# A hybrid block on one core: weights and small parameters laid out by the host, one piece per partition and transfer

## The chip, the core and the metric

The kernel runs on one core of a Trainium2 chip. The core has TensorE (PE in the profile), VectorE (DVE), ScalarE (ACT), GpSimd (POOL) and SyncE (SP), an on-chip memory of 128 partitions, an accumulation memory that PE writes, and 16 DMA engines that serve the transfers issued from the queues of SP, ACT and POOL. The metric is the device time of one execution in microseconds (us), the median over runs.

## The reference

A block of a diffusion transformer on 1024 latent tokens and 256 context tokens of width 1024, in float32. Cut to what matters:

```python
mod = silu(c) @ w_ada + b_ada                     # six rows of 1024: shift, scale, gate, twice
h = layer_norm(x) * (1 + sc1) + sh1               # the same for the context rows
proj = concat(h_ctx, h_x) @ w_in                  # 1024 x 3088: q, k, v, z, beta, decay, rx, ry
q, k, v = silu(conv4(q, k, v))                    # depthwise convolution over 4 tokens
o = gated_delta_rule(q, k, v, beta, decay)        # 4 heads, both directions, chunks of 64 tokens
hr = rg_lru(conv4(rx), wa, ba, wi, bi, lam)       # linear recurrence, both directions
u = concat(rmsnorm(o) * silu(z), hr * gelu(ry)) @ w_out
x = layer_norm(2**0.25 * x + gt1 * u) * g0 + b0
hm = layer_norm(x) * (1 + sc2) + sh2
y = sum over the two chosen experts e of 32:      # one group of four, then the top two in it
        weight[e] * (silu(hm @ gate[e]) * (hm @ up[e])) @ down[e]
out = layer_norm(2**0.25 * x + gt2 * y) * g1 + b1
```

The experts' weights are the bulk of what is read: 32 x (1024 x 256 gate, 1024 x 256 up, 256 x 1024 down), 96 MB.

## The kernel before, in words

One function, `hybrid_block`, builds the whole program. The order of the instructions on each engine is planned when the program is built, from a simulated timeline, and kept at run time.

**Head (0 to 85 us).** `c` and `c_ctx` are loaded as rows (L178, L179), passed through Silu, transposed by PE and copied to `cT`. `ada_rows` (L198) loads the first 2048 columns of `w_ada` in four transfers of 2 MB (tile `wada`, two buffers) and multiplies. The bias `b_ada` is loaded as rows `br` and transposed too (L213 to L217). The rows of x come on ACT's queue behind the third and fourth of these transfers. `wbd` (L239 to L241) holds 16 columns of `w_in` in 64-byte rows. Then come the layer norm, transposes and the split of h into a high and a low part (`hhi`, `hlo`). `stg` (L293 to L303) gathers 92 rows of small parameters in six transfers and transposes them into `par`; `dtb` (L305 to L307) takes two broadcasts.

**Projections, delta rule and recurrence (85 to 575 us).** `proj_cm` (L407) loads 128 columns of `w_in` (24 times 512 KB, in rows of 512 bytes), splits them and multiplies. `ada_late` loads the rest of `w_ada` in 32 transfers of 512 KB. `rg_gates` (L740) sets `wg` to zero on POOL and fills its diagonal blocks with four transfers, four times.

**Scan and output (575 to 853 us).** `prepare` (L925) loads `w_out` in eight transfers on SP's queue and after them the router's weights in two (L941, L942), the first with 16-byte rows, the second with 128-byte rows. `scan_step`, `rest` and `finish` run the delta rule over chunks, the output projection, the norms and the router's logits.

**Experts (853 to 1240 us).** Token and expert pairs are packed into 24 blocks of 128 places, of which some hold parts of two or four experts. For each block POOL gathers rows of `h2d` (L1449), PE transposes them, `up` (L1471) multiplies with gate and up side by side (`w`, 8 values of k, 512 columns), `down` (L1492) with the down weights (`d`), DVE scales the result into `y` (three buffers), and POOL adds it row by row into `acc` in DRAM (L1496): one scatter for each expert part of the block, 39 in all. Each of these scatters waits until the one before has landed, since they add into the same tensor. `load_w` (L1373) and `load_d` (L1380) bring the weights on SP's queue into six buffers for `w` and five for `d`; `behind` lets each load start only when the one two places before it has landed.

**End (1240 to 1279 us).** `acc` is read back, normalised and written out.

Of the kernel before, what the change touches and what calls it, by code (L numbers as in the profile page):

```python
# [9 lines left out]
F32 = mybir.dt.float32  # L10
# [8 lines left out]
P = 128  # L19
D = 1024  # L20
# [67 lines left out]
def hybrid_block(ctx, tc, x, c, ctx_in, c_ctx, w_ada, b_ada, w_in, conv_qkv_w, dn_a_log, dn_dt_bias, dn_onorm_w,  # L88
         rg_conv_w, rg_conv_b, rg_wa, rg_ba, rg_wi, rg_bi, rg_lambda, w_out, ln_g, ln_b,
         router_wg, router_bg, router_we, router_be, w_e_gate, w_e_up, w_e_down, ranks, only, out):  # L90
# [86 lines left out]
    cc = sb.tile([16, P], F32, name="cc", tag="cc")  # L177
    nc.sync.dma_start(cc[0:8, :], c[0].rearrange("(k p) -> k p", p=P))  # L178
    nc.sync.dma_start(cc[8:16, :], c_ctx.rearrange("(k p) -> k p", p=P))  # L179
# [14 lines left out]
    w_ada_v = w_ada[0].rearrange("(k p) n -> p k n", p=P)  # L194
# [45 lines left out]
    nc.vector.memset(wbd, 0.0)  # L240
    nc.scalar.dma_start(wbd[:, :, 0:16], w_in[0].rearrange("(k p) n -> p k n", p=P)[:, :, 2048:2064])  # L241
# [53 lines left out]
    nc.scalar.dma_start(stg[48:64, :], rg_conv_w[0].rearrange("j (t p) -> (j t) p", p=P))  # L295
    nc.scalar.dma_start(stg[64:68, :], rg_conv_b[0].rearrange("(t p) -> t p", p=P))
    nc.scalar.dma_start(stg[68:76, :], rg_ba[0].rearrange("d (t p) -> (d t) p", p=P))
    nc.scalar.dma_start(stg[76:84, :], rg_bi[0].rearrange("d (t p) -> (d t) p", p=P))
    nc.scalar.dma_start(stg[84:92, :], rg_lambda[0].rearrange("d (t p) -> (d t) p", p=P))
    pp = pm()  # L300
# [83 lines left out]
    w_in_v = w_in[0].rearrange("(k p) n -> p k n", p=P)  # L384

# [21 lines left out]
    def proj_cm(col, ctx_too):  # L407

        hi, lo = split_w(w_in_v[:, :, col:col + P], KT, P)
# [513 lines left out]
    w = {}  # L923
# [730 lines left out]
```

## Time and profile before

| | us |
|---|---|
| median of 3 runs | 1289.57 |
| lowest and highest of them | 1284.93, 1298.79 |
| the profiled execution | 1280.62 |
| its span, first to last instruction | 1278.9 |
| PE busy in it | 1112.5 (87%) |
| DVE busy | 682.3 (53%) |
| ACT busy | 422.4 (33%) |
| POOL busy | 424.9 (33%) |

The profile is one execution. A line of the timeline gives the start, the duration, engine, line of the program, operation, output and inputs, and in brackets how long the engine was idle before and what ended that. The chain of waits is followed back from the last instruction, at each step to what released it; "SPq" is a DMA issue on SP's queue, "issue" is time in which nothing that the profile shows was waited for. The share of the DMA engines is the sum of the packets' durations over 16 engines; it can come out a little above 1. q1 is SP's queue, q10 ACT's, q0 POOL's.

### The profile page before, as it was taken

What the parts mean: (1) busy time and instruction counts of PE and PEld (TensorE: products, weight loads), DVE (VectorE), ACT (ScalarE), POOL (GpSimd) and SP (SyncE); (2) the same over time, 40 slices, a digit from 0 to 9 for tenths busy, and PEclk for the clock granted to TensorE, in tenths of its full rate; (3) what the DMA queues carried; (4) which work ended last, traced back from release to release, by engine and by line L of the source; (5) the groups of instructions that cost most, each with busy time, mean ns of one, the idle gap of its engine ahead of it and who ended that gap; (6) DMA issues with size and microseconds to landing.
All of it is one profiled execution on the core that took longest, in us unless ns stands there. A gap on an engine that the chain in (4) does not pass through costs nothing.

```text
span 1278.9 us, 18429 instructions
## 1 busy us (share of the span) xinstructions
PE 1112.5 (87%) x6810; PEld 701.4 (55%) x6810; DVE 682.3 (53%) x1570; ACT 422.4 (33%) x755; POOL 424.9 (33%) x492
## 2 busy tenths in 40 slices
PE   4799998998999989987999999984898999999720
PEld 1357775776767677665667777772323433443210
DVE  3737479487684975875446766654211322222227
ACT  0535324233321727971222446540211212112003
POOL 1511414232242223353640176841211322222225
PEclk8799999999897999996999999975999999999975
DMA  9413453645536231009886255349999999999955
GB/s 335 163 49 93 140 149 94 189 139 140 141 111 160 69 104 37 17 19 306 266 256 214 93 188 185 114 186 332 336 332 355 342 309 307 308 311 315 314 178 169
DMA packets 208883, 251.43 MB, mean 197 GB/s; under 512 B 37276, under 2 KB 164440, under 8 KB 208792
## 3 DMA queue, kind: packets, MB, share of 16 engines
q1 hardware_dynamic: 194128, 215.94, 53.0%
q0 software_dynamic: 7888, 16.80, 5.7%
q10 hardware_dynamic: 6776, 17.50, 3.5%
q8 instruction: 54, 0.88, 0.3%
q14 instruction: 37, 0.30, 0.1%
HBM read 206.39 MB, written 55.20 MB: 205 GB/s over the span
## 4 chain that ended last, share of the span: by engine, by line
PE 39%; DMA 29%; DVE 17%; issue 6%; POOL 3%; SPq 3%; ACT 3%; DVEq 0%; POOLq 0%; ACTq 0%
DMA w<-in_w_e_up_dram 8%; DMA acc<-y,tbri 5%; PE pj L403 4%; PE pj L405 4%; PE pj L404 4%; DMA acc<-y,rows_to 4%; DMA d<-in_w_e_down_dram 4%; DVE s L621 4%; DVE s L619 4%; DMA wada<-in_w_ada_dram 2%; PE pu L1471 2%; PE p L1148 2%; PE pf L403 2%; PE pf L405 2%; PE pf L404 2%
## 5 line engine op out<-in xcount | busy, mean ns | idle before, releaser
L1471 PE MATMUL pu<-w,xT 128*32 128x512 f32 (+2 forms) x848 | 189.1, 614 | 19.0 <-DMA w<-in_w_e_up_dram 17.0
L403 PE MATMUL pj<-hhi,whi 128*128 128x512 f32 (+1 forms) x480 | 188.6, 393 | 4.5 <-ACT s L439 2.8
L404 PE MATMUL pj<-hlo,whi 128*128 128x512 f32 (+1 forms) x480 | 185.9, 387 | 0.0
L405 PE MATMUL pj<-hhi,wlo 128*128 128x512 f32 (+1 forms) x480 | 184.3, 385 | 0.0
L1471 PEld LDWEIGHTS pu<-w,xT 128*32 128x32 f32 (+2 forms) x848 | 61.8, 135 | 116.9 <-issue 104.0
L403 PEld LDWEIGHTS pj<-hhi,whi 128*128 128x128 f32 x480 | 92.5, 193 | 49.6 <-issue 18.6
L399 POOL TENSOR_TENSOR wlo<-wraw,whi 128x1024 fp32r<-128x1024 f32 x21 | 52.8, 2513 | 155.2 <-ACT whi L398 87.3
L405 PEld LDWEIGHTS pj<-hhi,wlo 128*128 128x128 f32 x480 | 92.7, 193 | 20.8 <-issue 5.7
L1492 PE MATMUL py<-d,hT 128*32 128x512 f32 (+2 forms) x424 | 101.0, 598 | 3.1 <-DMA d<-in_w_e_down_dram 2.1
L404 PEld LDWEIGHTS pj<-hlo,whi 128*128 128x128 f32 x480 | 92.8, 193 | 19.3 <-issue 5.3
L1474 DVE TENSOR_TENSOR hid<-hid,pu 128x256 f32<-128x256 f32 x24 | 10.0, 421 | 138.0 <-ACT hid L1473 138.0
L1496 POOL DMA_INDIRECT acc<-y,rows_to x28 | 41.3, 1476 | 116.4 <-DMA acc<-y,rows_to 51.0
L619 DVE TENSOR_TENSOR s<-s,s 80x31 f32<-80x31 f32 (+15 forms) x124 | 65.4, 527 | 14.4 <-DMA s<-ad 11.8
L434 DVE SCALAR_TENSOR_TENSOR cv<-pj,par,cv 128x504 f32<-128x504 f32 (+3 forms) x96 | 63.9, 668 | 11.3 <-ACT cv L422 10.3
L1493 DVE SCALAR_TENSOR_TENSOR y<-py,tbw,gt 128x512 f32<-128x512 f32 x48 | 35.7, 750 | 62.9 <-PE py L1492 52.8
L1462 ACT ACTIVATE xT<-pf,mod 128x128 f32<-128x128 f32 x96 | 37.8, 455 | 89.4 <-PE pf L1458 82.8
L1464 DVE TENSOR_SCALAR xT<-pf,mod 128x128 f32<-128x128 f32 x96 | 34.8, 405 | 59.4 <-ACT xT L1462 50.2
L1449 POOL DMA_INDIRECT xg<-h2d,tbri x24 | 25.4, 1060 | 117.4 <-PE pf L1458 69.8
L1492 PEld LDWEIGHTS py<-d,hT 128*32 128x32 f32 (+2 forms) x424 | 31.7, 131 | 57.3 <-issue 51.5
L621 DVE TENSOR_TENSOR s<-s,s 80x31 f32<-80x31 f32 (+15 forms) x124 | 61.9, 499 | 2.3
L1473 ACT ACTIVATE hid<-pu 128x256 f32<-128x256 f32 x24 | 9.1, 384 | 147.0 <-PE pu L1471 147.0
L403 PE MATMUL pf<-whi,yh 128*128 128x512 f32 x128 | 53.9, 421 | 1.9 <-DVE x L974 1.2
(483 smaller groups left out, 2123.1 us busy)
## 6 DMA issues: line engine op xcount, KB each, us to landing
w<-in_w_e_gate_dram SPq DMA_DIRECT2D x32, 1024.0 KB, 7.9
w<-in_w_e_up_dram SPq DMA_DIRECT2D x32, 1024.0 KB, 8.3
d<-in_w_e_down_dram SPq DMA_DIRECT2D x32, 1024.0 KB, 6.4
st<-sp SPq DMA_DIRECT2D x52, 384.0 KB, 5.2
wraw<-in_w_ada_dram SPq DMA_DIRECT2D x32, 512.0 KB, 4.6
wraw<-in_w_in_dram SPq DMA_DIRECT2D x24, 512.0 KB, 5.3
wada<-in_w_ada_dram SPq DMA_DIRECT2D x4, 2048.0 KB, 8.4
sp<-t SPq DMA_DIRECT2D x12, 512.0 KB, 4.6
```

The costliest lines, as they stand in the source:

```text
L399: (nc.vector if i in PA["LOV"] else nc.gpsimd).tensor_tensor(lo, raw, hi.bitcast(F32), op=ALU.subtract)
L403: nc.tensor.matmul(o, lh, rh, start=start, stop=False)
L404: nc.tensor.matmul(o, lh, rl, start=False, stop=False)
L405: nc.tensor.matmul(o, ll, rh, start=False, stop=stop)
L434: nc.vector.scalar_tensor_tensor(yo, xi, w(j), yo, op0=ALU.mult, op1=ALU.add)
L619: nc.vector.tensor_tensor(t_, sa[:, j + 1:32, j:j + 1].to_broadcast([80, n, j + 1]), T[:, j:j + 1, 0:j + 1].to_broadcast([80, n, j + 1]), ...
L621: nc.vector.tensor_tensor(T[:, j + 1:32, 0:j + 1], T[:, j + 1:32, 0:j + 1], t_, op=ALU.subtract)
L1462: nc.scalar.activation(self.xT[:, i, 0:u], pt[:, k * P:k * P + u], AF.Identity, bias=mod2[:, 0, i:i + 1], scale=mod2[:, 1, i:i + 1])
L1471: nc.tensor.matmul(pu[o:o + n, :], self.xT[:, k, o:o + n], ws[r][:, k, :], start=k == 0, stop=k == KT - 1)
L1492: nc.tensor.matmul(py[o:o + n, :], self.hT[:, f, o:o + n], ws[r][:, f, qs], start=f == 0, stop=f == 1)
L1493: nc.vector.scalar_tensor_tensor(y[0:u, qs], py[0:u, :], self.weights[0:u], gt2[0:u, qs], op0=ALU.mult, op1=ALU.mult)
L1496: nc.gpsimd.indirect_dma_start(out=acc, out_offset=bass.IndirectOffsetOnAxis(ap=to[0:o + n], axis=0), in_=y[0:o + n], in_offset=None, boun ...
```

## The change

The host lays the inputs out before the launch so that each transfer reads one contiguous piece per partition. `w_ada`'s first part becomes four tensors with 16 KB per partition, the rest 32 with 4 KB; the columns of `w_in` 24 with 4 KB; gate and up are joined per expert to 16 KB per partition and loaded in two halves of 8 KB, now by k (0 to 3, 4 to 7) where it was gate and up; the down weights have 8 KB per partition. The small parameters that were rows are one tensor `small_p` of 172 values per partition, loaded first on SP's queue, so that three transposes by PE and their copies fall away. `wbd`, `wg` and the router's weights come with their zeros or side by side, in one transfer each. What is computed is the same. The core of the diff:

```diff
-    cc = sb.tile([16, P], F32, name="cc", tag="cc")
-    nc.sync.dma_start(cc[0:8, :], c[0].rearrange("(k p) -> k p", p=P))
-    nc.sync.dma_start(cc[8:16, :], c_ctx.rearrange("(k p) -> k p", p=P))
+    sp_ = ca.tile([P, 172], F32, name="sp_")
+    nc.sync.dma_start(sp_, small_p)
+    bc_, par = sp_[:, 16:64], sp_[:, 64:156]
+    dtb = sp_[:, 156:172].rearrange("p (a f) -> p a f", a=2)
...
-    nc.scalar.activation(cc, cc, AF.Silu)
-    p0 = pm()
-    nc.tensor.transpose(p0[:, 0:16], cc, ident[0:16, 0:16])
     cT = ca.tile([P, KT, 32], F32, name="cT")
     nc.vector.memset(cT, 0.0)
-    nc.vector.tensor_copy(cT[:, :, 0:2], p0[:, 0:16].rearrange("p (s k) -> p k s", s=2))
+    nc.scalar.activation(cT[:, :, 0:2], sp_[:, 0:16].rearrange("p (k s) -> p k s", s=2), AF.Silu)
...
-        ada.append(nc.sync.dma_start(w, w_ada_v[:, :, n * 512:(n + 1) * 512]))
+        ada.append(nc.sync.dma_start(w, ada_first[n].rearrange("p (k c) -> p k c", k=KT)))
...
-    br = sb.tile([48, P], F32, name="br", tag="br")
-    nc.scalar.dma_start(br, b_ada[0].rearrange("(k p) -> k p", p=P))
-    nc.tensor.transpose(p0[:, 16:64], br, ident[0:48, 0:48])
-    bc_ = ca.tile([P, 48], F32, name="bc_")
-    nc.vector.tensor_copy(bc_, p0[:, 16:64])
...
-    nc.vector.memset(wbd, 0.0)
-    nc.scalar.dma_start(wbd[:, :, 0:16], w_in[0].rearrange("(k p) n -> p k n", p=P)[:, :, 2048:2064])
+    nc.scalar.dma_start(wbd, w_gates.rearrange("p (k c) -> p k c", k=KT))
...
-    stg = sb.tile([92, P], F32, name="stg", tag="stg")
-    nc.scalar.dma_start(stg[0:48, :], conv_qkv_w[0].rearrange("j (t p) -> (j t) p", p=P))
...
-    nc.tensor.transpose(pp[:, 0:92], stg, ident[0:92, 0:92])
-    par = ca.tile([P, 92], F32, name="par")
-    nc.vector.tensor_copy(par, pp[:, 0:92])
-    dtb = ca.tile([P, 2, 8], F32, name="dtb")
-    nc.scalar.dma_start(dtb[:, 0, :], dn_dt_bias[0:1].rearrange("o d h -> o (d h)").to_broadcast([P, 8]))
-    nc.scalar.dma_start(dtb[:, 1, :], dn_a_log[0:1].rearrange("o d h -> o (d h)").to_broadcast([P, 8]))
...
-        hi, lo = split_w(w_in_v[:, :, col:col + P], KT, P)
+        i = col // P if col < 2048 else (col - 16) // P
+        hi, lo = split_w(w_cols[i].rearrange("p (k c) -> p k c", k=KT), KT, P)
...
-                s = nc.sync.dma_start(w, w_ada_v[:, 2 * q:2 * q + 2, 2048 + n * 512:2560 + n * 512])
+                s = nc.sync.dma_start(w, ada_rest[4 * n + q].rearrange("p (k c) -> p k c", k=2))
...
-        nc.gpsimd.memset(wg, 0.0)
-        for gi, src in enumerate((rg_wa, rg_wi)):
-            for e in range(2):
-                nc.sync.dma_start(wg[64 * e:64 * e + 64, gi, :, 64 * e:64 * e + 64],
-                                  src[0, :, 2 * j + e].rearrange("d c f -> c d f"))
+        nc.sync.dma_start(wg, rg_w[j].rearrange("p (g d c) -> p g d c", g=2, d=2))
...
-        nc.sync.dma_start(w["r"][:, :, 0:4], router_wg[0].rearrange("(k p) g -> p k g", p=P))
-        nc.sync.dma_start(w["r"][:, :, 4:36], router_we[0].rearrange("(k p) e -> p k e", p=P))
+        nc.sync.dma_start(w["r"], router_w.rearrange("p (k e) -> p k e", k=KT))
...
-        behind(nc.sync.dma_start(w[:, :, 0:256], w_e_gate[0, sl].rearrange("o (k p) f -> p (o k) f", p=P)), after)
-        behind(nc.sync.dma_start(w[:, :, 256:512], w_e_up[0, sl].rearrange("o (k p) f -> p (o k) f", p=P)), None)
+        src = w_up[sl].rearrange("o p (k f) -> p (o k) f", k=KT)
+        for q in range(2):
+            behind(nc.sync.dma_start(w[:, 4 * q:4 * q + 4, :], src[:, 4 * q:4 * q + 4, :]), None if q else after)
...
-        behind(nc.sync.dma_start(w, w_e_down[0, bass.ds(e, 1)].rearrange("o (k p) f -> p (o k) f", p=P)), after)
+        behind(nc.sync.dma_start(w, w_down[bass.ds(e, 1)].rearrange("o p (k f) -> p (o k) f", k=2)), after)
...
+def by_partition(a, k):
+    return np.ascontiguousarray(np.asarray(a).reshape(k, P, -1).transpose(1, 0, 2).reshape(P, -1))
```

## Rows read from the trace of the kernel before

**Rows 1.** Stretches: us, busy per engine (instructions), PE clock, DMA share, GB/s.

```profile
0.00:45.00 45.00, 26.35 (x121) 10.61 (x122) 19.20 (x55) 7.72 (x13) 8.27 (x32) 0.77 0.89 322
...
85.00:560.00 475.00, 450.80 (x2854) 336.17 (x2853) 337.13 (x676) 206.97 (x286) 148.43 (x94) 0.96 0.40 111
560.00:625.00 65.00, 56.77 (x322) 41.30 (x321) 36.05 (x81) 18.18 (x25) 34.91 (x32) 0.84 0.71 223
...
888.00:1225.00 337.00, 311.38 (x1512) 119.56 (x1510) 82.57 (x178) 56.47 (x145) 77.58 (x58) 0.98 0.99 319
```

**Rows 2.** Waits, 885 to 1240 us: engine line <- releaser: us, times, longest.

```profile
POOL acc L1496 <- DMA acc<-y,rows_to: 82.0, 19, 9.4
...
POOL acc L1496 <- DMA acc<-y,tbri: 48.3, 8, 8.3
...
PE pu L1471 <- DMA w<-in_w_e_up_dram: 17.0, 7, 5.5
```

**Rows 3.** Timeline of PE, experts: start, us, instruction, [idle before <- releaser].

```profile
924.35 12.70 PE L1471 MATMUL pu<-w,xT 128*32 128x512 f32 x96 [5.54 <-DMA w<-in_w_e_up_dram]
...
951.77 7.07 PE L1471 MATMUL pu<-w,xT 128*32 128x512 f32 x62 [1.44 <-DMA w<-in_w_e_up_dram]
960.56 7.10 PE L1471 MATMUL pu<-w,xT 128*128 128x512 f32 x16 [1.72 <-DMA w<-in_w_e_up_dram]
...
982.68 8.67 PE L1492 MATMUL py<-d,hT 128*32 128x512 f32 x64 [1.31 <-DMA d<-in_w_e_down_dram]
...
1195.42 8.13 PE L1471 MATMUL pu<-w,xT 128*64 128x512 f32 x29 [4.76 <-DMA w<-in_w_e_up_dram]
```

**Rows 4.** Timeline of POOL, experts: three scatters into acc.

```profile
987.42 1.34 POOL L1496 DMA_INDIRECT acc<-y,rows_to  x1 [14.03 <-DVE y L1493]
...
1208.48 1.43 POOL L1496 DMA_INDIRECT acc<-y,rows_to  x1 [8.73 <-DVE y L1493]
...
1221.32 1.43 POOL L1496 DMA_INDIRECT acc<-y,rows_to  x1 [5.48 <-DVE y L1493]
```

**Rows 5.** Chain that ended last, experts: start, us, what.

```profile
1205.87 2.38 issue
...
1219.12 1.96 issue
```

**Rows 6.** DMA queue q1 in 943-957, 25-30, 1240-1248 us: packets, MB, share.

```profile
q1 hardware_dynamic: 3901, 3.93, 87.0%
...
q1 hardware_dynamic: 775, 1.58, 83.0%
...
q1 hardware_dynamic: 875, 3.20, 100.0%
```

**Rows 7.** Timeline of SP's queue: first and last of 28 gate and up issues.

```profile
852.93 0.42 SPq L1376 DMA_DIRECT2D w<-in_w_e_gate_dram  x1
...
973.18 0.37 SPq L1377 DMA_DIRECT2D w<-in_w_e_up_dram  x1
```

**Rows 8.** Scatters (L1496) landing in 986-1210, 1207-1219, 1219-1240 us.

```profile
DMA to landing us min/median/max: 4.7/7.3/10.2
...
DMA to landing us min/median/max: 4.8/5.2/5.5
...
DMA to landing us min/median/max: 4.4/4.5/6.0
```

**Rows 9.** Chain that ended last, head: start, us, what.

```profile
3.27 15.26 DMA wada<-in_w_ada_dram
...
22.27 10.08 DMA wada<-in_w_ada_dram
```

**Rows 10.** Timeline, head: first product with w_ada.

```profile
10.10 3.64 PE L208 MATMUL pm<-wada,cT 128*32 128x512 f32 x16 [4.87 <-DMA wada<-in_w_ada_dram]
```

**Rows 11.** Chain that ended last, change-over: SP's queue at the router weights.

```profile
592.80 2.38 SPq L941
...
595.22 3.38 SPq L942
```

More of the change, by code (lines that the diff above doesn't have):

```diff
@@ L87, in hybrid_block @@
 @with_exitstack
-def hybrid_block(ctx, tc, x, c, ctx_in, c_ctx, w_ada, b_ada, w_in, conv_qkv_w, dn_a_log, dn_dt_bias, dn_onorm_w,
-         rg_conv_w, rg_conv_b, rg_wa, rg_ba, rg_wi, rg_bi, rg_lambda, w_out, ln_g, ln_b,
-         router_wg, router_bg, router_we, router_be, w_e_gate, w_e_up, w_e_down, ranks, only, out):
+def hybrid_block(ctx, tc, x, ctx_in, small_p, ada_first, ada_rest, w_cols, w_gates, rg_w, dn_onorm_w, w_out, ln_g, ln_b,
+         router_w, router_bg, router_be, w_up, w_down, ranks, only, out):
     nc = tc.nc
@@ L185, in later @@
         return s
-    nc.scalar.activation(cc, cc, AF.Silu)
-    p0 = pm()
-    nc.tensor.transpose(p0[:, 0:16], cc, ident[0:16, 0:16])
     cT = ca.tile([P, KT, 32], F32, name="cT")
     nc.vector.memset(cT, 0.0)
-    nc.vector.tensor_copy(cT[:, :, 0:2], p0[:, 0:16].rearrange("p (s k) -> p k s", s=2))
-    w_ada_v = w_ada[0].rearrange("(k p) n -> p k n", p=P)
+    nc.scalar.activation(cT[:, :, 0:2], sp_[:, 0:16].rearrange("p (k s) -> p k s", s=2), AF.Silu)
     ada = []
@@ L291, in hybrid_block @@
     nc.vector.tensor_copy(bd, pb[:, 0:160].rearrange("p (t f) -> p t f", f=16))
-    stg = sb.tile([92, P], F32, name="stg", tag="stg")
-    nc.scalar.dma_start(stg[0:48, :], conv_qkv_w[0].rearrange("j (t p) -> (j t) p", p=P))
[L295 to L300, printed above, removed]
-    nc.tensor.transpose(pp[:, 0:92], stg, ident[0:92, 0:92])
-    par = ca.tile([P, 92], F32, name="par")
-    nc.vector.tensor_copy(par, pp[:, 0:92])
-    dtb = ca.tile([P, 2, 8], F32, name="dtb")
-    nc.scalar.dma_start(dtb[:, 0, :], dn_dt_bias[0:1].rearrange("o d h -> o (d h)").to_broadcast([P, 8]))
-    nc.scalar.dma_start(dtb[:, 1, :], dn_a_log[0:1].rearrange("o d h -> o (d h)").to_broadcast([P, 8]))
     def softplus(o, v, n):
@@ L382, in g5 @@
         return sb.tile([P, n], F32, name=tag, tag=tag, bufs=bufs)
-    w_in_v = w_in[0].rearrange("(k p) n -> p k n", p=P)
     unit = [0]
@@ L1624, in hybrid_block @@
                 nc.sync.dma_start(out[0, c0:c0 + 64, :], x_[64 * b:64 * b + 64, :])
-_INS = ['x', 'c', 'ctx', 'c_ctx', 'w_ada', 'b_ada', 'w_in', 'conv_qkv_w', 'dn_a_log', 'dn_dt_bias', 'dn_onorm_w',
-        'rg_conv_w', 'rg_conv_b', 'rg_wa', 'rg_ba', 'rg_wi', 'rg_bi', 'rg_lambda', 'w_out', 'ln_g', 'ln_b',
-        'router_wg', 'router_bg', 'router_we', 'router_be', 'w_e_gate', 'w_e_up', 'w_e_down']
+def by_partition(a, k):
+    return np.ascontiguousarray(np.asarray(a).reshape(k, P, -1).transpose(1, 0, 2).reshape(P, -1))
@@ new lines, in layout @@
+def layout(i):
+    i = {k: np.asarray(v) for k, v in i.items()}
+    ada, w_in = i['w_ada'][0], i['w_in'][0]
+    col = lambda a: a.reshape(-1, P).T
+    c = np.stack([col(i['c'][0]), col(i['c_ctx'])], axis=2).reshape(P, 16)
+    gates = np.stack([i['dn_dt_bias'][0].reshape(8), i['dn_a_log'][0].reshape(8)]).reshape(1, 16)
+    small = [c, col(i['b_ada'][0])] + [col(i[n][0]) for n in ('conv_qkv_w', 'rg_conv_w', 'rg_conv_b', 'rg_ba', 'rg_bi', 'rg_lambda')]
+    rg = np.zeros((4, 2, 64, 2, 2, 2, 64), dtype=np.float32)
+    for g, n in enumerate(('rg_wa', 'rg_wi')):
+        for j in range(4):
+            for e in range(2):
+                rg[j, e, :, g, :, e, :] = i[n][0, :, 2 * j + e].transpose(1, 0, 2)
+    blocks = [k * P if k < 16 else 16 + k * P for k in range(24)]
+    bd = np.zeros((D, 32), dtype=np.float32)
+    bd[:, 0:16] = w_in[:, 2048:2064]
+    up = np.concatenate([i['w_e_gate'][0], i['w_e_up'][0]], axis=2)
+    pack = lambda a, k: a.reshape(32, k, P, -1).transpose(0, 2, 1, 3).reshape(32, P, -1)
+    return {
+        'x': i['x'], 'ctx': i['ctx'],
+        'small_p': np.concatenate(small + [np.repeat(gates, P, axis=0)], axis=1),
+        'ada_first': np.stack([by_partition(ada[:, n * 512:(n + 1) * 512], KT) for n in range(4)]),
+        'ada_rest': np.stack([by_partition(ada[256 * q:256 * q + 256, 2048 + n * 512:2560 + n * 512], 2) for n in range(8) for q in range(4)]),
+        'w_cols': np.stack([by_partition(w_in[:, b:b + P], KT) for b in blocks]),
+        'w_gates': by_partition(bd, KT),
+        'rg_w': rg.reshape(4, P, 512),
+        'dn_onorm_w': i['dn_onorm_w'], 'w_out': i['w_out'], 'ln_g': i['ln_g'], 'ln_b': i['ln_b'],
+        'router_w': by_partition(np.concatenate([i['router_wg'][0], i['router_we'][0]], axis=1), KT),
+        'router_bg': i['router_bg'], 'router_be': i['router_be'],
+        'w_up': pack(up, KT), 'w_down': pack(i['w_e_down'][0], 2),
+    }
@@ L1641 @@
     arrays, args = {}, []
-    for name in _INS + list(_CONSTS):
-        a = np.ascontiguousarray(_CONSTS[name] if name in _CONSTS else inputs[name])
+    for name, a in {**layout(inputs), **_CONSTS}.items():
+        a = np.ascontiguousarray(a)
         arrays[f"in_{name}_dram"] = a
```

## The prediction

> **What bounds the kernel now.** I read the table of stretches first [rows 1]. It cuts the span into a head (0 to 45 us), the projections and the delta rule (85 to 560), a change-over (560 to 625), the scan (625 to 853, not shown) and the experts (888 to 1225). The reader is to compare two columns. From 85 to 560 PE is busy 450.8 of 475 us and DMA has a share of 0.40: a faster transfer meets an engine that is not waiting for it. In the head DMA has 0.89, in the experts 0.99, with PE at 311.4 of 337: only there do the weights and PE stand close together. Nearly all that the change can move is there.
>
> Second, in the experts, the waits by engine [rows 2]. PE waits for gate and up weights 17.0 us in all, in seven places. That is about the ceiling of what PE itself can win. But POOL, which issues the 39 scatter-adds into acc, waits 82.0 + 48.3 us for the scatter before to land, at 27 of them. Third, PE's timeline says where those 17 us are: 5.54 us at 924.35, 1.44 at 951.77, 1.72 at 960.56, 1.31 (down weights) at 982.68, together 10.0 us, and 4.76 at 1195.42 [rows 3]; the rest is small. Fourth, POOL's timeline [rows 4]: up to 987.42 a scatter waits for its data (14.03 us for DVE's y). After that only the two at 1208.48 and 1221.32 do; the others wait for the scatter ahead, or for a gather that POOL issues between and that itself starts about when the scatter ahead lands. The chain of waits says how much slack there is at these two: 2.38 and 1.96 us [rows 5]. So there are two regimes: until about 987 weights set the pace, from 987 to 1237 the chain of scatters does, at (1208.5 - 987.4) / 27 = 8.2 us each [rows 4], while PE runs just ahead of it.
>
> **The change part by part.** *Expert weights.* Before, gate and up came as two transfers of 1 MB whose rows per partition and k are 1 KB; after, two transfers of 1 MB with 8 KB per partition; the down weights go from 4 KB to 8 KB rows. Number, order and spacing of the issues stay. Price of a packet: in a stretch with gate and up alone, queue q1 moved 3901 packets in 87.0% of 16 engines for 14 us, so 16 x 14000 x 0.87 / 3901 = 50 ns for 1 KB. The 2 KB rows of the head: 16 x 5000 x 0.83 / 775 = 86 ns. The 4 KB rows of the end: 16 x 8000 / 780 (875 less 95 tiny ones) = 164 ns [rows 6]. No row shows 8 KB; from 2 KB to 4 KB it is 78 ns more, so I estimate 164 + 2 x 78 = 320 ns, against 8 x 50 = 400 for the same bytes in 1 KB rows. A 1 MB transfer is 64 KB for each of 16 engines, 8 such packets: 0.64 us saved; beside other traffic all packets are dearer, so I take 0.5 us, bounds 0.2 and 0.65. From 4 KB to 8 KB it is (2 x 164 - 320) x 8 = 0.06 us: nothing.
>
> By 973.18, 28 gate and up transfers have been issued since 852.93 [rows 7]: 14 by the wait at 924.35 (7 us saved against 5.54 waited), 28 by that at 982.68 (14 us against 10.0). So all four waits go: the chain of scatters is fed 10 us earlier. The new halves are by k instead of gate and up, so PE's first four k of a block need only the first half; that covers up to half a block (3.6 us) of what would still be late. After 987 the weights come 0.5 us sooner each, but what is late next is the scatter: the chain keeps its 27 x 8.2 us and moves as a whole. At its end the 2.38 and 1.96 us of waiting for data may go too, since PE's wait at 1195 is for weights [rows 3]; I take half, 2 us. Experts: -12 us; bounds -19 (all PE waits, a shorter scatter) and the rival below.
>
> What do 8 KB packets do to the scatters? A scatter lands in 7.3 us (median of 28) with gate, up and down loads around it, in 5.2 (of two) where only the 4 KB down loads are left, in 4.5 (of three) where none is [rows 8]. Load costs up to 2.8 us, yet the stretch with fourfold rows is not the worst one. The least price is a gain (fewer packets, and the engines are no longer full: -0.5 us each), the most is that the load's 2.8 us grow with the packet. Nearest row is the 5.2: I take 0. The Trainium skill, DMA: Bandwidth & Descriptors, section "Queues, rings and completion order", says that a DMA engine serves its queues in turn and changes over only at the end of a packet. By that rule a scatter row would wait behind longer packets, and the sum would be the slower rival's below; the 5.2 us beside 7.3 does not bear it out so far.
>
> *Head.* Four transfers of 2 MB go from 2 KB to 16 KB rows: 4096 x 86 / 16 = 22.0 us of engine time becomes 512 x (164 + 6 x 78) / 16 = 20.2. The 1024 tiny packets of wbd and those of the parameter rows cost some 0.7 us and become 128 each. Two of these transfers are pieces of the chain, 15.26 and 10.08 us long [rows 9], so I take it all: -2.5 us. Bounds 0 and -6 (the last one shares the engines with rows of x; 2 MB alone, at the 1.58 MB / (5 us x 0.83) = 381 GB/s of its own packets, would be 5.5 us [rows 6]). New is that Silu waits for small_p, 88 KB in one transfer, where it waited for two of 4 KB, ahead of the weights on SP's queue; queued behind it on ACT are the table loads and on PE the first product. That product starts at 10.10 after 4.87 us of idle, waiting for its weights [rows 10]: this is the cover. Without it the price would be about the transfer's 0.3 us. The two transposes of the parameters, their copies and memsets and nine small issues on ACT's queue fall into the same cover or, for stg after the head, cost PE one small product: nothing.
>
> *Router weights.* Their two issues hold SP's queue 2.38 and 3.38 us [rows 11], with w_out's next load behind them. One issue of 128 rows should hold it 0.4 us, as the weights' do [rows 7]: 5.4 us earlier. PE is busy 56.8 of 65 us there [rows 1], with other work to do, so I take -2; bounds 0 and -5.4.
>
> *Projections.* The 24 column loads go from 512-byte to 4 KB rows and land sooner; the rg gates lose four memsets and 12 of 16 issues. Cover is PE, busy 450.8 of 475 us [rows 1]. I take 0; bounds +3 (the order of the instructions is planned from transfer costs and may come out otherwise) and -3.
>
> **Sum:** -12 - 2.5 - 2 + 0 = -16.5 us. The profiled execution took 1280.6 us (span 1278.9) and would take 1264. The median of the runs shown is 1289.57, 0.7% above it; the same cut gives 1273.
>
> **The rivals.** *The scatters slow down* (slower). Place: POOL's chain from 987 on, 27 scatters. Price: the 2.8 us that load adds [rows 8] grow by half or more, since each row of a scatter meets an 8 KB packet where it met 1 or 4 KB: 1.4 x 27 = 38 us, less 16.5, so +21 and 1311 us. For it: the chain has no slack, so each tenth counts 27 times. Against: the 5.2 us. It decides from (16.5 + 13) / 27 = 1.1 us per scatter on.
>
> *It is hidden.* The scatters or PE eat the lead: PE's 10 us before 987 come back as waits for y buffers (there are three), or the weights stay at 3.93 MB / (14 us x 0.87) = 323 GB/s because something else than the packets limits them. Then head and router remain, and a few us: -4, so 1286 us. For it: PE is at 311 of 337 [rows 1]. Against: the 4 idle places are clearly weights [rows 3], and 2 KB rows already reach 381 GB/s [rows 6].
>
> *Transfers are the bound after all.* 56 gate and up transfers after 888 at 0.5 us are 28 us; with head and router -33, so 1257 us. For it: share 0.99 [rows 1]. It needs scatters that get shorter by 0.6 us once the engines are less full [rows 8]; PE's 19 us of waits speak against the whole of it.
>
> *The change does not do what it says*: 8 KB rows are cut up on the way to 4 KB packets. Then 0.57 instead of 0.64 us are saved: no other time.
>
> **How the numbers follow.** Forecast (-8 to -25 us) 0.50, hidden (-8 to +8) 0.27, transfers the bound (beyond -25) 0.09, slower scatters 0.14. About 1% (12.9 us) is what a measurement of this kernel can tell from no change: under 1276.7 is faster, over 1302.5 slower. Of the forecast's 0.50 some 0.38 lie beyond -12.9. Faster: 0.38 + 0.09 = 0.47; slower: the rival's part from 1.1 us on, 0.13; the rest, 0.40, is the same. The range takes in the forecast, the hidden case and a part of both ends, leaving out 0.1 on each side: 1254 to 1302; the forecast's own is 1264 to 1282.
>
> **What would show it.** Right: some 61,000 packets fewer in the experts (57,344 of gate and up, 4,096 of down); PE's waits for w gone before 980; POOL's first scatter that waits for the one before it in an unbroken run at about 977 less what head and router gave; scatters landing in 7.3 us. Wrong: a median landing over 8.4 us (slower scatters), DVE's waits for acc over 20 us (hidden), router issues over 1 us, or an order of PE's blocks or of the scan that differs from before.

## The result, and the profile after

The changed kernel is slower. Nine executions of it gave 1304.86 us (median, 1294.32 to 1313.42), nine of the kernel before 1287.2 us (1281.33 to 1298.79): a ratio of 1.0137, 95% interval 1.0107 to 1.0166, some 17.6 us more where 16.5 us less were forecast. A later pair gave 1.0134, interval 1.0099 to 1.0170. The profiled execution of after took 1306.3 us with a span of 1304.4.

The table of stretches comes first, as [rows 1] did (columns as there; the last row is the experts, from PE's first gate and up product to its last product):

```profile
0.00:45.00 45.00, 29.77 (x127) 12.58 (x128) 23.70 (x60) 8.36 (x14) 10.51 (x35) 0.70 0.88 345
85.00:560.00 475.00, 457.01 (x2862) 339.53 (x2862) 329.11 (x663) 204.42 (x281) 145.81 (x88) 0.95 0.37 111
560.00:625.00 65.00, 48.95 (x264) 34.06 (x262) 40.38 (x73) 25.47 (x32) 35.20 (x31) 0.79 0.57 185
897.00:1236.00 339.00, 319.50 (x1508) 119.95 (x1506) 80.86 (x176) 56.51 (x145) 73.05 (x55) 0.98 0.93 316
```

Two rows matter here. From 560 to 625 PE is busy 48.95 of 65 us, where it was 56.77: the change-over lost PE time. In the experts the DMA share fell from 0.99 to 0.93, and the rate stayed at 316 GB/s (319 before): the engines got idle time, and the weights did not come faster.

Next the waits in the experts, 893 to 1265 us (engine, line <- releaser: us, times, longest), against [rows 2]:

```profile
POOL acc L1464 <- DMA acc<-y,rows_to: 112.0, 23, 9.3
...
POOL acc L1464 <- DMA acc<-y,tbri: 68.7, 8, 10.8
```

POOL waits for the scatter ahead 112.0 + 68.7 us, where it was 82.0 + 48.3. The group of the scatters on the page says the same (busy us, mean ns of one | idle of POOL before them), first before, then after:

```profile
L1496 POOL DMA_INDIRECT acc<-y,rows_to x28 | 41.3, 1476 | 116.4 <-DMA acc<-y,rows_to 51.0
```
```profile
L1464 POOL DMA_INDIRECT acc<-y,rows_to x28 | 41.3, 1475 | 144.6 <-DMA acc<-y,rows_to 67.5
```

Issuing a scatter costs what it did (1475 ns); POOL's idle time before it is 28 us longer. The scatters of [rows 8] landed in 7.3 us (median); those that start between 986 and 1220 us in after land in:

```profile
DMA to landing us min/median/max: 6.3/8.7/11.7
```

How the chain runs is read off POOL's timeline. Of the 39 scatters these are the 5th and the 33rd, before and then after (start, us, [idle before]), and the last of after:

```profile
953.63 1.44 POOL L1496 DMA_INDIRECT acc<-y,rows_to  x1 [3.11 <-DMA acc<-y,rows_to]
...
1193.25 1.33 POOL L1496 DMA_INDIRECT acc<-y,rows_to  x1 [6.08 <-DMA acc<-y,tbri]
```
```profile
961.97 1.43 POOL L1464 DMA_INDIRECT acc<-y,rows_to  x1 [5.56 <-DMA acc<-y,rows_to]
...
1226.25 1.33 POOL L1464 DMA_INDIRECT acc<-y,rows_to  x1 [10.43 <-DMA acc<-y,tbri]
...
1256.84 1.56 POOL L1464 DMA_INDIRECT acc<-y,tbri  x1 [3.93 <-DMA acc<-y,rows_to]
```

Twenty-eight steps took (1193.25 - 953.63) / 28 = 8.56 us each before, (1226.25 - 961.97) / 28 = 9.44 us after. This spacing, from the 5th scatter to the 33rd, is the yardstick below. (The forecast's 8.2 us ran from the 8th to the 35th.)

The other loss lies ahead of the experts. PE's longest waits from 560 to 612 us, first before, then after:

```profile
PE p L1136 <- DMA st<-spc: 4.2, 1, 4.2
PE p L1118 <- DVE S L1155: 3.0, 2, 1.9
PE p L1148 <- DVE vn L1139: 0.5, 1, 0.5
```
```profile
PE p L1115 <- DVE vn L1106: 7.5, 2, 7.3
PE p L1085 <- DVE S L1122: 3.7, 2, 3.2
PE p L1103 <- DMA st<-spc: 3.2, 2, 2.7
```

The wait for vn, 0.5 us before, is 7.5 us. DVE's timeline tells why; again before, then after:

```profile
573.75 2.37 DVE L814 TENSOR_TENSOR PT<-PT,cv 128x512 f32<-128x512 f32 x2 [2.59 <-POOL PT L795]
582.13 0.61 DVE L1139 TENSOR_SCALAR vn<-p,scol 128x128 f32<-128x128 f32 x2 [6.01 <-PE p L1136]
```
```profile
586.25 1.73 DVE L782 TENSOR_TENSOR PT<-PT,cv 128x512 f32<-128x512 f32 x1 [2.55 <-DMA st<-spc]
587.91 0.60 DVE L1106 TENSOR_SCALAR vn<-p,scol 128x128 f32<-128x128 f32 x2
```

Before, the last products of the recurrence's output (PT) were off DVE's list 6 us ahead of the first vn. After, PT stands in front of vn: the last product of the recurrence's gates ends at 570.4 us instead of 561.9, and the scan's first step waits behind its tail. Seen over the whole stretch, from the end of the last projection product to the end of the last scan product, before takes 818.22 - 576.60 = 241.6 us and after 827.98 - 577.02 = 251.0 us (ends of the last products in PE's timeline). Nearly 10 us are lost there. The three waits shown make 7.7 us before and 14.4 after, 6.7 us of them; the granted clock from 560 to 625 us is lower too (0.79 against 0.84), and what that costs wasn't separated.

### The profile page after: what moved, and what is told of

It reads as the page before. It is cut to its first block, busy times and chain, and to the rows that moved or that the text cites. A ratio compares the mean times of both kernels' runs of the same rounds, so it can differ in the third digit from the quotient of the medians.

```text
span 1304.4 us, 18355 instructions
## 1 busy us (share of the span) xinstructions
PE 1132.2 (87%) x6807; PEld 706.0 (54%) x6807; DVE 683.9 (52%) x1566; ACT 429.1 (33%) x760; POOL 428.1 (33%) x488
## 5 line engine op out<-in xcount | busy, mean ns | idle before, releaser
L374 PE MATMUL pj<-hhi,whi 128*128 128x512 f32 (+1 forms) x480 | 192.4, 401 | 3.3 <-ACT s L411 3.3
L1460 PE MATMUL py<-d,hT 128*32 128x512 f32 (+2 forms) x424 | 110.8, 616 | 2.8 <-DMA d<-in_w_down_dram 2.4
L1464 POOL DMA_INDIRECT acc<-y,rows_to x28 | 41.3, 1475 | 144.6 <-DMA acc<-y,rows_to 67.5
L591 DVE TENSOR_TENSOR s<-s,s 80x31 f32<-80x31 f32 (+15 forms) x124 | 61.6, 497 | 20.0 <-DMA s<-ad 17.6
L406 DVE SCALAR_TENSOR_TENSOR cv<-pj,sp__81,cv 128x504 f32<-128x504 f32 (+3 forms) x96 | 64.1, 668 | 9.5 <-ACT cv L394 8.4
```

The lines of the kernel that those rows point to most:

```text
L374: nc.tensor.matmul(o, lh, rh, start=start, stop=False)
L406: nc.vector.scalar_tensor_tensor(yo, xi, w(j), yo, op0=ALU.mult, op1=ALU.add)
L591: nc.vector.tensor_tensor(t_, sa[:, j + 1:32, j:j + 1].to_broadcast([80, n, j + 1]), T[:, j:j + 1, 0:j + 1].to_broadcast([80, n, j + 1]), ...
L1460: nc.tensor.matmul(py[o:o + n, :], self.hT[:, f, o:o + n], ws[r][:, f, qs], start=f == 0, stop=f == 1)
L1464: nc.gpsimd.indirect_dma_start(out=acc, out_offset=bass.IndirectOffsetOnAxis(ap=to[0:o + n], axis=0), in_=y[0:o + n], in_offset=None, boun ...
```

## The experiments

In the tables "spacing" is the yardstick above, "idle" POOL's idle time before its 28 scatters into rows_to (page, group of the scatters), "landing" the median of scatters that start from 986 to 1210 us, "scan" the stretch from the last projection to the last scan product.

### Expert weights: length of rows, and the rest apart

The first and second run lay gate and up out apart, so that only the length of rows changes, and the planned order on every engine stays that of before (2 KB shown; 8 KB is the same with one group of eight k):

```diff
-        w = place("w", [P, KT, 512], i, 2)
+        w = place("w", [P, 2, KT, 256], i, 2)
-        behind(nc.sync.dma_start(w[:, :, 0:256], w_e_gate[0, sl].rearrange("o (k p) f -> p (o k) f", p=P)), after)
+        wv = w.rearrange("p a (g t) f -> p a g (t f)", t=2)
+        behind(nc.sync.dma_start(wv[:, 0, :, :], w_g8[sl].rearrange("o (g p) f -> p (o g) f", p=P)), after)
...
-                    nc.tensor.matmul(pu[o:o + n, :], self.xT[:, k, o:o + n], ws[r][:, k, :], start=k == 0, stop=k == KT - 1)
+                    nc.tensor.matmul(pu[o:o + n, :].rearrange("p (a f) -> p a f", a=2), self.xT[:, k, o:o + n], ws[r][:, :, k, :], start=k == 0, stop=k == KT - 1)
```

> Only the gate and up weights are laid out anew, gate and up apart, so that each partition's piece of a half is one row of 8 KB (1 KB eight times before); the two transfers of an expert stay gate and up, and the planned order on all five engines is that of the kernel before, row for row. The kernel before takes about 1287 us. Theory A (long rows of weights delay the rows of the scatters, the scatter chain stretches): +9 to +15 us, 1296 to 1302, with no change of the first product of the experts (889 us) and the last scatter over 20 us behind the last down product (8 us before). Theory B (the loss at the experts comes from the halves by k and the order planned anew): 1287 or, with the waits for weights gone, 1277 to 1287. My prediction before the result would have said 1277.

> As the run with 8 KB rows, with rows of 2 KB (two k together): the same bytes, transfers and order. Theory A: the delay of a scatter's row goes with the time of one weight packet, which is 84 ns at 2 KB in the trace of before against 50 ns at 1 KB and 355 ns at 8 KB in the trace of after, so about a ninth of the loss at 8 KB, +1 to +2 us, or less than nothing if the shorter list of packets frees time: 1283 to 1289. Theory B: 1287 or a little less, as for 8 KB.

The third takes from the change only load_d:

```diff
-        behind(nc.sync.dma_start(w, w_e_down[0, bass.ds(e, 1)].rearrange("o (k p) f -> p (o k) f", p=P)), after)
+        behind(nc.sync.dma_start(w, w_down[bass.ds(e, 1)].rearrange("o p (k f) -> p (o k) f", k=2)), after)
```

> Only the down weights are laid out anew, in rows of 8 KB (two of 4 KB before); order as before. Theory A: a third of the bytes moves from packets of 159 to packets of 309 ns, which is a third of the traffic times half of the packet time of the 8 KB case: +2 to +4 us, 1289 to 1291. Theory B: 1287.

The fourth is the change with load_w and load_d as before.

> All of the change but the expert weights (parameters, modulation, projection, gate and router weights laid out anew; expert weights as before). Theory C (about 10 of the 18 us are lost between the recurrence and the scan, where the instructions come in another planned order): the last scan product at 826 to 829 us instead of 818, the experts as long as before, 1295 to 1299 in all. Rival D (the 10 us come from the longer rows or from chance differences between executions): 1283 to 1288, last scan product at 816 to 820.

```
                       ratio   95% interval      spacing  idle   landing
gate, up 8 KB          0.9982  0.9944 to 1.0020  9.07     135.5  8.4
gate, up 2 KB          0.9999  0.9968 to 1.0031  8.81     118.0  7.6
down 8 KB              1.0001  0.9966 to 1.0036  8.82     121.2  7.5
all but the experts    1.0026  0.9994 to 1.0059  8.86     114.3  8.5
```

The +9 to +15 us for long rows did not come: no single part costs what the whole does. Still 8 KB rows of gate and up stretch the chain (9.07 us), and PE's waits for w are shorter there (9.2 us where [rows 2] has 17.0); that this loss and this gain cancel is my reading. Theory C holds in the trace (last scan product at 826.5 us, scan 251.6 us), but its cost in time, 0.26%, is not clear of nothing here, where 8 to 12 us were expected.

### Halves by k, and both kinds of expert weights

```diff
         sl = bass.ds(e, 1)
+        src = w_up[sl].rearrange("o p (k f) -> p (o k) f", k=KT)
+        for q in range(2):
+            behind(nc.sync.dma_start(w[:, 4 * q:4 * q + 4, :], src[:, 4 * q:4 * q + 4, :]), None if q else after)
```

This is the change's load_w (the fifth run). The sixth differs by `"o (k p) f -> p (o k) f", p=P`, the seventh adds load_d of the third, the eighth joins the first and the third.

> Gate and up weights as in the changed kernel: one tensor, two transfers of four k each, rows of 8 KB; the rest as before. Against the run with 8 KB rows and gate and up apart (1289 us, no difference from before) this adds the halves by k and the order that the planner then makes for the experts (3 rows of PE's list fewer, 7 places at the experts differ). Theory E (the planned order at the experts, with the halves by k, makes the loss): +10 to +15 us, 1299 to 1304. Theory F (gate/up and down rows of 8 KB are harmless each and cost together): 1289. Theory G (the loss comes only where the later start of the experts and the new rows meet): 1289.

> As the run before it, instruction for instruction in the same order on every engine, but gate and up weights lie in rows of 2 KB. Theory E: as the run with 8 KB rows, 1299 to 1304. Rival (rows of 8 KB are needed too): 1289, with the 8 KB run at 1299 or more. Theories F and G: 1289.

> Both expert parts of the changed kernel, gate/up halves by k and down weights in 8 KB rows; everything ahead of the experts in the order of before. Theory E: as halves by k alone, 1299 to 1304. Theory F: 1299 to 1304, where halves by k alone give 1289. Theory G: 1289 to 1292.

> Gate, up and down weights all in rows of 8 KB, gate and up apart, and so in the order of before on every engine. Theory E: 1289. Theory F: 1299 to 1304. Theory G: 1289.

```
                       ratio   95% interval      spacing  idle   landing
halves by k, 8 KB      1.0017  0.9974 to 1.0061  9.30     143.3  9.7
halves by k, 2 KB      1.0031  0.9993 to 1.0068  8.84     142.9  7.2
both expert parts      1.0044  1.0009 to 1.0078  9.57     149.9  9.3
both, order of before  1.0044  1.0010 to 1.0078  9.34     143.0  9.5
```

Theory E falls: halves by k and the order that goes with them cost at most a little, though the 1.0031 of the sixth run can't be told from 1.0044 with these intervals. Both kinds in 8 KB rows are slower by 0.44%, with the order of before (eighth run) as with the new one, so the rows make this loss without the new order; of theory F's +10 to +15 us about 6 came. Idle is no clean sign (142.9 with 2 KB rows and the new order), landing not quite one (8.5 in the fourth run, 8.4 in the first); spacing is.

### Second traces of before and after, and the largest rows

> The kernel before, unchanged, for a second trace: it tells which differences between two traces are those of single executions. The first trace's span (1278.9 us) lies 8 us under the median of its kernel (1287 to 1291), and the scatters followed each other there at 8.56 us on average. Theory A' (long rows slow the scatter chain, but the first trace of before was taken on a good execution): 8.6 to 8.9 us from scatter to scatter again, below the 9.07 to 9.57 of the runs with 8 KB rows. Rival (the spacing differs that much from execution to execution whatever the rows): 9.0 or more. The last scan product at 817 to 821 us either way.

> The changed kernel, unchanged, on the same chip as the other runs of this call, and a second trace of it. If its two sides simply add (all but the experts 1.0026, experts 1.0044): a ratio of 1.005 to 1.010. If they make each other worse: 1.011 to 1.017 as at first. Its trace: last scan product at 826 to 829 us again if the planned order is the cause, and 9.3 to 9.6 us from scatter to scatter if the long rows are.

The eleventh run has gate and up in one row of 16 KB, two transfers of 64 partitions each, and the down rows of 8 KB; the sixteenth one transfer of 128 partitions. It stands twice in the list that `behind` counts, so that no two of these 2 MB transfers are open together:

```diff
+        for q in range(2):
+            behind(nc.sync.dma_start(w[64 * q:64 * q + 64], src[64 * q:64 * q + 64]), None if q else after)
```
```diff
+        s = nc.sync.dma_start(w, w_up[sl].rearrange("o p (k f) -> p (o k) f", k=KT))
+        behind(s, after)
+        loads.append(s)
```

> The largest dose: gate and up weights of an expert in one row of 16 KB per partition, the two transfers taking 64 partitions each; down weights in rows of 8 KB; all ahead of the experts as in before, and the order nearly so (3 places in PE's list). Theory A' (a scatter's rows wait behind one weight packet each, and the scatter chain ends the kernel): 10 us or more from scatter to scatter, and 1300 to 1315 us. Rival (what hurts is only the changed order or chance): 1287 to 1297 and at most 9.4 us from scatter to scatter.

> Gate and up weights of an expert in one transfer over all 128 partitions, rows of 16 KB; down weights in rows of 8 KB; all ahead of the experts as in before, the order at the experts near that of the halves by k. Theory A' (a scatter's rows wait behind single weight packets): the 16 KB packets take 600 to 750 ns under load (8 KB: 355), the scatters stand 10.2 to 10.8 us apart, 1300 to 1315 us. Rival (8 KB rows cost something else, and packet length does nothing more): 9.3 to 9.8 us apart, 1292 to 1300 us. If the 16 KB packets take 1200 ns here too, it is their length and not the 64 partitions that slowed run 11.

```
                          ratio   95% interval      spacing  landing  scan
before again              1.0020  0.9988 to 1.0052  8.86     8.2      241.0
changed again             1.0134  1.0099 to 1.0170  9.83     9.1      251.5
16 KB, 64 partitions      1.1123  1.1084 to 1.1162  12.89    9.6      243.5
16 KB, 128 partitions     1.0262  1.0204 to 1.0321  9.76     8.0      243.7
```

The second trace of before settles how far one execution can be trusted: its span is 1288.9 us against 1278.9, its spacing 8.86 against 8.56. Over all traces the two kinds keep apart: eleven with gate and up in 1 or 2 KB rows lie between 8.56 and 8.86 us, seven with 8 KB between 9.07 and 9.83. The largest dose is a miss. With 64 partitions to a transfer the transfers themselves became the bound (stretches of 889 to 987 and 987 to 1354 us, columns as in [rows 1]):

```profile
889.00:987.00 98.00, 58.22 (x278) 19.93 (x274) 13.42 (x30) 12.06 (x29) 11.16 (x9) 0.79 0.98 227
987.00:1354.00 367.00, 272.45 (x1219) 101.15 (x1218) 63.39 (x141) 42.91 (x112) 58.12 (x43) 0.88 1.00 238
```

227 to 238 GB/s at a share of 0.98 to 1.00: that run tells nothing of the scatters. Over 128 partitions, 889 to 987 and 987 to 1236 us:

```profile
889.00:987.00 98.00, 79.08 (x398) 27.96 (x396) 16.91 (x40) 15.24 (x38) 17.67 (x14) 0.92 0.81 294
987.00:1236.00 249.00, 224.84 (x1077) 86.64 (x1074) 62.27 (x133) 39.61 (x103) 52.59 (x39) 0.98 0.89 305
```

The spacing stayed at 9.76 us instead of 10.2 to 10.8, and landings got no longer (8.0 us). The packets did: from 1100 to 1110 us queue q1 moved (columns as in [rows 6]; 64 partitions, then 128)

```profile
q1 hardware_dynamic: 165, 2.18, 97.5%
...
q1 hardware_dynamic: 267, 3.01, 79.1%
```

which is 16 x 10000 x 0.975 / 133 = 1170 ns for each 16 KB over 64 partitions and 16 x 10000 x 0.791 / 184 = 690 ns over 128, so the length of the rows alone is not what slowed the eleventh run. PE is busy 79 of 98 us at the start, where the two 8 KB traces of both expert parts have 88 to 89 of 97 to 99; and the 8th scatter starts at 1009.5 us instead of 984 to 992. So most of the 34 us (2.62%) is lost at the start; that PE waits there for whole transfers fits, but was not tested by itself. That every scatter row waits behind one whole packet of weights, so that twice the row costs twice the delay, isn't borne out.

### The order ahead of the scan

The twelfth run takes only the gate weights of the recurrence from the change, the fifteenth all but those and the experts:

```diff
-        nc.gpsimd.memset(wg, 0.0)
-        for gi, src in enumerate((rg_wa, rg_wi)):
-            for e in range(2):
-                nc.sync.dma_start(wg[64 * e:64 * e + 64, gi, :, 64 * e:64 * e + 64],
-                                  src[0, :, 2 * j + e].rearrange("d c f -> c d f"))
+        nc.sync.dma_start(wg, rg_w[j].rearrange("p (g d c) -> p g d c", g=2, d=2))
```

> Only the recurrence's gate weights are laid out anew: one transfer per j in place of four, no clearing of wg. The planner then puts the last product of these gates at place 1751 of PE's list (before 1717, all parts 1754). Theory C' (this moves the loss ahead of the scan): last gate product at 568 to 571 us (before 560 to 562), last scan product at 825 to 829 (before 814 to 820). Rival (the parameters and the other parts moved it): 560 to 563 and 817 to 821. Time: 1290 to 1297 by the first, 1286 to 1291 by the second.

> All but the experts and the recurrence's gate weights. Theory C' (the gate weights' one transfer makes the order that loses time): last gate product at 560 to 564 us, last scan product at 813 to 819, and with the head's 2.6 us kept 0.996 to 1.000. Rival (the parameters of the head make it): 567 to 571, 824 to 828, and 1.003 to 1.007.

The seventeenth takes only modulation and projection weights (the order of before on all engines), the eighteenth these and the parameters:

```diff
-                s = nc.sync.dma_start(w, w_ada_v[:, 2 * q:2 * q + 2, 2048 + n * 512:2560 + n * 512])
+                s = nc.sync.dma_start(w, ada_rest[4 * n + q].rearrange("p (k c) -> p k c", k=2))
...
-        hi, lo = split_w(w_in_v[:, :, col:col + P], KT, P)
+        hi, lo = split_w(w_cols[i].rearrange("p (k c) -> p k c", k=KT), KT, P)
```

> Modulation weights (both stages) and projection weights laid out anew, rows of 1 or 2 KB joined to 4 to 16 KB; expert weights, gate weights and parameters as before. The planned order on all five engines is that of before. If the order makes the loss ahead of the scan: last scan product at 814 to 820 us, a PE wait of about 4 us at the change to the scan, not 7 to 10; and if the head's 2.6 us come from the modulation weights, they show (last of their products at 33 to 34 us), 0.996 to 1.001 in all. If the new layout itself costs there: last scan product at 824 or later, 1.003 to 1.007.

> As the run before it, with the parameters in one piece and no transposes in the head, which plans the whole kernel anew; PE's planned order at the change from recurrence to scan stays that of before, the recurrence's gate products come 13 places later. If what matters is the order at that change: last scan product at 813 to 820, 0.994 to 1.000. If any new order loses as much: 824 to 828, 1.003 to 1.007.

```
                          ratio   95% interval      scan   last scan product
rg gate weights alone     1.0072  1.0044 to 1.0099  256.8  823.7
rest without rg, experts  1.0044  1.0011 to 1.0077  248.8  826.0
layout, order of before   0.9992  0.9963 to 1.0021  244.5  825.7
layout and parameters     0.9987  0.9952 to 1.0022  245.2  824.0
```

The gate weights alone show the wait of after, PE's waits from 560 to 612 us:

```profile
PE p L1142 <- DVE vn L1133: 7.3, 1, 7.3
```

The fifteenth run, without them, does not have it, but one of 9.5 us of another kind, as has the eighteenth, whose row this is:

```profile
PE p L1107 <- DMA st<-spc: 9.5, 1, 9.5
```

Thirteen traces with the order of before ahead of the experts take 240.9 to 245.0 us for the stretch, five with the gate weights laid out anew 251.0 to 256.8. By the marks of its expectation the fifteenth run went the rival's way: 1.0044, last gate product at 565.3 us, last scan product at 826.0. In the seventeenth the absolute time of the last scan product misled: it came at 825.7 us with the old order, because that execution was 3.8 us late at its first column product already (74.4 us against 70.6) and 4.6 at its last. (DVE waited 7.0 us there for rows of x, 2.2 in both traces of before; one trace doesn't tell whether by chance.) Its scan took 244.5 us like the others. So the gate weights alone are enough for the loss, by the wait for vn. They are not the only way to it: without them the fifteenth kernel still takes 4 to 8 us more for the stretch and is slower by 0.44%. The eighteenth, which leaves the router's weights and `wbd` as before too, shows neither (245.2 us, 0.9987); those two parts weren't run by themselves. Neither the seventeenth nor the eighteenth is measurably faster than before.

### Do the parts add up?

Both halves of the change (the seventh and the fourth kernel) again, with more executions.

> Both expert parts of the change alone, again. If the parts add up to the whole: a ratio of 1.006 to 1.009. If they make each other worse: 1.002 to 1.005. Scatters 9.3 to 9.8 us apart either way (before 8.6 to 8.9).

> All but the experts, again. If the parts add up: 1.004 to 1.007 (experts begin 7 to 8 us later, scatters 8.6 to 8.9 us apart). If they make each other worse: 1.000 to 1.003.

```
                       ratio   95% interval      spacing  scan
both expert parts      1.0064  1.0030 to 1.0099  9.34     243.2
all but the experts    1.0053  1.0023 to 1.0082  8.70     254.4
```

0.64% and 0.53% make 1.17%, the whole is 1.34 to 1.37%, each with an interval of about a third of a per cent to either side. So the parts can make up the whole: some 8 us from the expert weights, some 7 from what lies ahead of them. The first values of the same two kernels, 0.44% and 0.26%, make only 0.70%; each lies inside the interval of the second. So an effect of the one on the other isn't needed, but one of a few us isn't ruled out.

## Why the prediction was wrong, point by point

**Expert weights, the 10 us before 987.** This is the first step that failed. The packet was priced nearly right. In 14 us with gate and up (951 to 965), queue q1 moved (packets, MB, share of 16 engines, as [rows 6]):

```profile
q1 hardware_dynamic: 581, 4.23, 84.3%
```

4.23 MB / 8192 are 516 packets, so 16 x 14000 x 0.843 / 516 = 366 ns, against 320 estimated and 400 for the same bytes before. That is 0.27 us a transfer, inside the bounds. But the transfers hardly came sooner. SP's queue, first and last issues of the same 28 (start, us):

```profile
862.18 1.26 SPq L1345 DMA_DIRECT2D w<-in_w_up_dram  x2
...
941.37 40.41 SPq L1345 DMA_DIRECT2D w<-in_w_up_dram  x12
```

From 862.2 to about 981.4 are 119 us for 28 issues, where [rows 7] has 120.3 (122.5 in the second trace of before). Over all traces it is 118.1 to 123.3 us with 8 KB rows (seven, mean 120.1) and 120.2 to 124.5 with rows of 1 or 2 KB (eleven, mean 122.7): 2.5 us sooner where 14 were expected. The engine time saved became idle time of the engines (share 0.93 instead of 0.99). From 850 to 1000 us SP's issues waited 97.2 us in all for an earlier load of weights to land (106.4 before), so the landings set their pace; why these came no sooner stays open, and more open transfers than the two that `behind` allows weren't tried. Accordingly the first scatter of the unbroken run comes 100.3 us after the first product of the experts (897.59 to 997.89), against 97.9 before (889.51 to 987.42) and 101.8 in the second trace of before; over the same traces the means are 99.0 and 102.0 us, 3 us of the 10. PE's waits for gate and up did shrink over the whole stage, 17.0 us in [rows 2] to

```profile
PE pu L1439 <- DMA w<-in_w_up_dram: 7.3, 2, 4.3
```

but the chain of scatters ends the stage, so what PE gains after 987 is worth nothing there. It is the rival *it is hidden*, in its second form, and later on in its first: DVE, which fills the three y buffers, waits for scatters to free them, first before (885 to 1240 us), then after (893 to 1265 us):

```profile
DVE y L1493 <- DMA acc<-y,tbri: 9.4, 3, 6.4
```
```profile
DVE y L1461 <- DMA acc<-y,rows_to: 27.5, 5, 11.8
...
DVE y L1461 <- DMA acc<-y,tbri: 25.0, 4, 7.6
```

That is 52.5 us for 9.4; over all traces 34 to 67 us with 8 KB rows (seven), 1 to 30 with gate and up in 1 or 2 KB (eleven).

**8 KB packets beside scatters, "I take 0".** The second failed step. The bounds were -0.5 and +1.4 us a scatter. Landings rose from medians of 7.2 to 8.5 us (eleven traces, the down weights alone among them) to 8.4 to 9.7 (seven), about 1.3 us, and the spacing by about 0.4 us with gate and up alone and 0.8 with the down weights too. The scatters' own packets did not get slower. From 990 to 1215 us queue q0 moved, first before, then after:

```profile
q0 software_dynamic: 5184, 12.00, 24.0%
```
```profile
q0 software_dynamic: 4768, 11.05, 21.3%
```

For 4 KB that is 16 x 225000 x 0.240 / 2930 = 295 ns before and 16 x 225000 x 0.213 / 2698 = 284 ns after. So the added 1.3 us are not in the packets themselves; that they are spent waiting behind packets of weights fits, but no row shows it. The nearest row, 5.2 us beside 4 KB rows, was no evidence for 8 KB: only down loads ran there, so less traffic and longer rows came together. The rival *the scatters slow down* had the mechanism and the place; its price was too high. Twenty-seven times 1.4 counted each landing in full, and it forgot the end: the last six steps took 1231.20 - 1193.25 = 38.0 us before, when they waited for data, and 1256.84 - 1226.25 = 30.6 us after, when the data lay ready. What remains is some 13 us from the 8th scatter to the last in the traces (mean 248 us in the eleven with gate and up in 1 or 2 KB rows, 261 in the five with both kinds in 8 KB), less the 3 us by which the chain starts sooner, and 6 to 8 us in the times; the 2 to 4 us between aren't explained.

The page's rule that I set beside it (the Trainium skill, DMA: Bandwidth & Descriptors, section "Queues, rings and completion order": an engine serves its queues in turn and changes at the end of a packet) pointed the right way. What that section calls a packet is a group of descriptors, typically 9 to 17; that it is what the profile counts as one packet isn't shown. The runs agree with its direction from 1 to 8 KB; the run with 16 KB rows and landings of 8.0 us doesn't agree with a delay in proportion to the row.

**Head, -2.5 us.** This step failed too: the gain came, and was given back. The last modulation product, then the first of the projections, first before, then after:

```profile
32.49 3.64 PE L208 MATMUL pm<-wada,cT 128*32 128x512 f32 x16 [2.47 <-DMA wada<-in_w_ada_dram]
...
70.55 0.39 PE L403 MATMUL pj<-hhi,whi 128*128 128x256 f32 x1
```
```profile
29.91 3.64 PE L204 MATMUL pm<-wada,cT 128*32 128x512 f32 x16
...
70.86 0.38 PE L374 MATMUL pj<-hhi,whi 128*128 128x256 f32 x1
```

2.6 us sooner at 30 us, 0.3 us later at 70. Over all traces the first of these starts at 31.9 to 33.7 us in the fourteen with the parameters as before and at 29.4 to 30.6 in the six with them in one piece, the second at 68.1 to 74.4 and 69.0 to 70.9. What failed is that the end of the modulation products would bring the end of the head. PE's last wait ahead of the projections, first before, then after:

```profile
54.00 1.97 PE L274 MATMUL pm<-ident,xt 128*128 128x128 f32 x8 [4.59 <-DVE xt L265]
```
```profile
55.41 1.91 PE L273 MATMUL pj<-hf,wbd 128*32 128x512 f32 x2 [2.40 <-ACT hf L266]
```

Before, PE waits for rows of x that DVE normalises (done at 53.9 us). After, DVE is done with them at 49.5 us, but PE waits for ACT's `hf` until 55.4; from 58 us on PE has no gap in either. The gain at 30 us comes with the parameters and not with the longer rows alone: with the modulation rows alone the last product ends at 36.2 us (before 36.1), with the parameters too at 34.2. The parameters without the longer rows weren't run.

**Router weights, -2 us.** The issue itself shrank:

```profile
600.11 0.96 SPq L909 DMA_DIRECT2D wr<-in_router_w_dram  x1
```

0.96 us for 2.38 + 3.38. By itself it wasn't run; in the new order w_out's first load is issued at 593.7 us (before 583.4), so nothing of it shows in w_out.

**Projections, "I take 0; bounds +3".** The third failed step. The reason was named (the order is planned from transfer costs) and then priced as if PE's cover held. It does, up to 560 us; but a plan that differs by a few places there ends with PT ahead of vn on DVE, and in the change-over nothing covers it: 8 to 13 us in the five traces with the gate weights in one transfer (the 13 in one whose projections ended 6 us earlier than in any other), 0.3 to 0.7% in the times.

**The sum, as the runs have it:** expert weights some 8 us more instead of 12 less, head and router nothing instead of 4.5 less, order some 7 more instead of nothing; 15 us by the later values of the parts, 17 by the whole. I held the two slower cases against each other as rivals, where the one (time saved and hidden) and the other (slower scatters) came together, and gave the order no case of its own.

**The signs of being wrong** read as they should: the median landing went over 8.4 us (8.7), DVE's waits for acc over 20 us (52.5), and the order of the scan differed. Two losses showed at once, and each was seen without the other (eighth and twelfth run). Of the signs of being right only the packets came: q1 moved 14,112 from 850 to 1245 us, 62,042 fewer than before. PE's waits for w before 980 did not go (3.01 us at 928.38, 4.29 at 959.80), and the unbroken run began at 997.9 us.

## What to carry to other kernels

Engine time saved on a transfer is only worth something if the transfer is what the next one waits for: look at the distance of the issues, not at the DMA share. Before long rows are put next to a serial chain of small transfers, measure the chain's step beside them; here 0.4 to 0.8 us at each of 28 steps was more than the longer rows gave. And where a planner orders the instructions, a change of layout is also a change of order: read the new order at the change of stages, where no other work covers a wait, and time the parts that keep the old order by themselves.

## What the runs showed of the hardware

Two transfers of 64 partitions and 16 KB rows ran at 227 to 238 GB/s with the engines full, one of 128 partitions at 294 to 305 with a share of 0.81 to 0.89; the time went up by 11% against 2.6%. The first had two such transfers open at a time, the second one of twice the size, so the partitions are not the only difference. The Trainium skill, DMA: Bandwidth & Descriptors, section "Rules for kernel authors", asks for 128 partitions for the most bandwidth, and these two rows agree. Two traces of one kernel, before, lie 10 us apart in span and 0.3 us in the scatters' step, as much as half of what was looked for; only the many traces side by side kept the kinds of rows apart.
